# Holding the next head group's features behind the current group's triangular inverse

## The chip, the cores and the metric

The kernel runs on one core of a Trainium2 chip. The metric is the device time of one execution in microseconds, as the median of several runs; the times and the profile of the kernel before are shown below. Of the engines, TensorE is PE in the profile (its weight loads are PEld), VectorE is DVE, ScalarE is ACT, GpSimd is POOL and SyncE is SP.

## What is computed

The reference is a chain of two two-layer blocks on 256 tokens of width 1024. The change lies in the first block's second layer, a linear-attention mixer (RWKV) over 256 context tokens and then 256 latent tokens, in two directions:

```python
def wkv_scan(s0, decay, k, v, kk, a, r, reverse):
    def step(S, inp):
        w_t, k_t, v_t, kk_t, kka_t = inp[:5]
        S = (S * w_t[:, :, None, :]
             - jnp.einsum('bhij,bhj->bhi', S, kk_t)[..., None] * kka_t[:, :, None, :]
             + v_t[..., None] * k_t[:, :, None, :])
        y = jnp.einsum('bhij,bhj->bhi', S, inp[5]) if emit else None
        return S, y
```

with `decay = exp(-exp(-softplus(-w_raw) - 0.5))`, `a` a sigmoid of a low-rank product, 16 heads of width 64, and the scan of the context run first, so that its last state starts the scan of the latent tokens.

## The kernel before

The scan is done in blocks of 64 tokens, four to a sequence. There are four **head groups** g = 0 to 3: context of heads 0 to 7, latent tokens of the same heads, context of heads 8 to 15, latent tokens of those. Each group goes through four stages.

**Features** (`rw_feat`, L1079), in eight units: four head pairs hp by two directions d. A unit makes two low-rank products on PE (L1098), two tanh on ACT, then the decay sums L, a running sum of log decays on DVE (the scan at L1107), and from L the exponentials E3 and E2 (L1112, L1114, ACT). With them DVE builds the scaled keys BK (L1133, L1134) and queries ARx or ARc (L1136 to L1139). PE transposes BK (L1155), ACT copies that and its queue sends it to DRAM (kbd), PE multiplies BK by AR (L1165), and DVE masks the products into the group's matrix tile AB (L1178 for latent, L1183 for context groups); latent groups also make RB (L1181) and a bonus term (L1145 to L1150), and send ARx and RB to DRAM. In what follows a unit of a latent group is an x unit, one of a context group a c unit.

**Inverse** (`rw_inv`, L1194). It needs all eight units. ACT copies the diagonal 32 by 32 blocks of AB into ND (L1201, four copies), DVE transposes them (L1202), and then 31 dependent pairs of DVE instructions (L1210 multiply into xtmp, L1211 add into X) invert 64 triangular blocks at once. `F["inv"]` is the last of them.

**Post** (`rw_post`, L1214; `rw_post2`, L1242, for the last group). Two DVE transposes of X (L1219, L1221), ACT copies, and 32 by 32 matmuls on PE (L1231, L1237) finish the inverse of the 64 by 64 blocks, in two halves.

**Chain** (`rw_chain`, L1274). Four steps s. A step needs the state St of the step before and the finished AB: PE makes pR (L1303, L1310, in `begin`), ACT copies it to rhs (L1323), PE multiplies by AB to pU (L1329), ACT copies to UV (L1333), PE makes the next state (L1350), DVE scales it to St (L1357); latent groups also make the output pY. The last step of a group makes the pR of the next group's first step. Key blocks, and for latent groups ard and rbd, come back from DRAM for each step.

Between these, `tick` (L339) places **ticks** on PE: two matmuls of a modulation product for the second block (L247, `ada_wide`), each with a load of 512 KB of weights (wraw, issued from SP into two buffers). Ticks are anchored behind feature products and pU products, and come one after another in program order.

In the loop at L943 the code of a group is written as inverse, post, chain, and `ahead(p)` writes the units of the next group at the chain steps in `pos`. That is the order in which they are written. The order in which each engine runs them is set when the kernel is built, by a scheduler that may place an instruction earlier if its inputs and buffers are there. `self.after(i, prev)` is an edge that it must keep: i stands behind prev on its engine, or waits for it.

Of the kernel before, what the change touches and what calls it, by code (L numbers as in the profile page):

```python
# [13 lines left out]
ALU = mybir.AluOpType  # L14
# [6 lines left out]
S = 256  # L21
# [745 lines left out]
class L1(K):  # L767
# [14 lines left out]
    def odd1(self, xs, cst, Acol, Bcol):  # L782

        nc, A, tc = self.nc, self.A, self.tc
# [5 lines left out]
        J, mstrict, mincl, rmask = rc[:, 0:P], rc[:, P:P + 64], rc[:, P + 64:2 * P], rc[:, 2 * P:]  # L790
# [22 lines left out]
        for d in range(2):  # L813
            nc.gpsimd.memset(E3[d][:, :, 64 * d:64 * d + 1], 1.0)
        bon = self.T(rk, [P, 2, 16], "bon")
        E = dict(E3=E3, kT=kTd, kkn=kknd, rT=rTd, twl=twl, tal=tal, hpar=hpar, hka=hka, vd=vd, ms=mstrict, mi=mincl, rmask=rmask, bon=bon, rkI=rkI,
                 kbd=[self.tc.dram_tile([2, 4, P, 4, P], F32, name=f"kb_dram{g}") for g in range(4)],
                 ard=[self.tc.dram_tile([2, 4, P, 4, P], F32, name=f"ar_dram{g}") for g in range(2)],
                 rbd=[self.tc.dram_tile([2, 4, P, 8, 64], F32, name=f"rb_dram{g}") for g in range(2)])
        self.weights(2)  # L820
        with self.phase(ns2=6) as ph:
# [72 lines left out]
            F = self.rw_open(0, False, fp, fw)  # L894
# [38 lines left out]
        with self.phase((3, 2, 1), 0) as ph:  # L933
            self.pl = ph.es.enter_context(tc.tile_pool(name="pl", bufs=1, space=PSUM, reuse_waits="tile"))
            gp = ph.pool("gp")
            St = [self.T(gp, [P, 2, 4, P], f"St{c}") for c in range(2)]
            for c in range(2):
                nc.gpsimd.memset(St[c], 0.0)
            E.update(St=St, yd=yd, Y1=Y1)
            self.lo = "lo"  # L940
            self.at, self.side = "unit", self.late_side
            st = None
            for g in range(4):  # L943
                N = {"hp": 0}

                def ahead(p):

                    while g < 3 and N["hp"] < 4 and self.pos[g][N["hp"]] <= p:
                        if N["hp"] == 0:
                            N["F"] = self.rw_open((g + 1) // 2, g % 2 == 0, fp if g == 2 else gp, gp)  # L950
                        self.rw_feat(N["hp"], gp, E, N["F"])
                        N["hp"] += 1
                ahead(0)
                self.rw_inv(gp, F)
                ahead(1)
                rest = (self.rw_post2 if g >= self.g2 else self.rw_post)(gp, F)
                st = self.rw_chain(gp, E, F, st, ahead, rest)
                ahead(9)
                F = N.get("F")
                if F:  # L960
                    Fl = F
            F = Fl

            self.do(self.side)
            E.update(z=z, J=J, sgl=sgl, behind=F["inv"])
            sl = slice(512, 1024)
            nc.gpsimd.dma_start(lng1, A["lng"][sl].partition_broadcast(P))
            nc.gpsimd.dma_start(g21, A["g2"][:, sl])
            t2 = lambda n: self.T(gp, [P, 512], n, bufs=3 if n in ("BK", "ARx") else 2)
            lng, lnb, g2 = (t2("BK") for _ in range(3))  # L970
            nc.gpsimd.dma_start(lng, A["lng"][0:512].partition_broadcast(P))
            nc.gpsimd.dma_start(lnb, A["lnb"][0:512].partition_broadcast(P))
            nc.gpsimd.dma_start(g2, A["g2"][:, 0:512])
            for t in range(2):
                rows = slice(t * P, (t + 1) * P)
                y, y1 = t2("KB"), t2("ARx")
                nc.scalar.dma_start(z[:, t, :], vd[0][rows, 0:512])
                nc.scalar.dma_start(y, yd[0][rows, :])
                nc.scalar.dma_start(y1, yd[1][rows, :])
                self.rw_bonus(0, t, E, z[:, t, :], lnb)  # L980
                self.rw_readout(t, E, y, y1, t2("RB"), lng, g2, z[:, t, :])
            lnb = t2("BK")
            nc.gpsimd.dma_start(lnb, A["lnb"][sl].partition_broadcast(P))
            for t in range(2):
                nc.scalar.dma_start(z1[:, t, :], vd[0][t * P:(t + 1) * P, sl])
                self.rw_bonus(1, t, E, z1[:, t, :], lnb)
# [92 lines left out]
    def rw_feat(self, hp, gp, E, F):  # L1079
        nc = self.nc  # L1080
# [14 lines left out]
        for d in range(2):  # L1095
            pwa = self.T(self.pl, [P, 2, S], self.lo)
            for n, (w2, l) in enumerate(((w2s, E["twl"]), (a2s, E["tal"]))):
                i = mm(pwa[:, n, :], w2[:, hp, :], l[:, d, tok], start=True, stop=True)  # L1098
            self.tick(self.tk[0][F["g"]][d], i)
            tw = f1()  # L1100
# [3 lines left out]
            rev = slice(None, None, -1) if d else slice(None)  # L1104
            nc.scalar.activation(tw, tw, AF.Copy, bias=-0.5 * DT_C, scale=-0.5 * DT_C)
            L = f1()
            nc.vector.tensor_tensor_scan(L[:, rev], E["rmask"][:, 0:S], tw[:, rev], 0.0, ALU.mult, ALU.add)  # L1107
            E3 = E["E3"][d]
            lo, hi = (1, 65) if d == 0 else (0, 64)
            plo, phi = (0, 64) if d == 0 else (1, 65)  # L1110
# [51 lines left out]
            for c in range(4):  # L1162
                for h2 in range(2):
                    hs = slice(64 * h2, 64 * h2 + 64)
                    i = mm(pxs[h2][:, c, :], BK[hs, c, :], ar[hs, c, :], start=True, stop=True)  # L1165
# [1025 lines left out]
```

## Time and profile before

| | |
|---|---|
| median of 3 runs | 2179.67 us (2177.97 to 2191.19) |
| the profiled execution's own time | 2203.59 us |
| its span, first to last instruction | 2201.8 us |
| PE busy in the span | 2014.0 us (91%) |
| DVE busy | 1216.7 us (55%) |
| ACT busy | 832.7 us (38%) |
| mean granted TensorE clock | 0.929 of full speed |

The four groups' inverses, posts and chains take the stretch from 880.8 to 1238.0 us of the span. The first eight units are made earlier, behind other layers' matmuls. In the profile's windows one sees busy time by engine; a busy PE includes the latency of each matmul, so that a stretch of small dependent matmuls shows a busy PE too. PEclk is the share of full clock that was granted: 1.00 is 2.4 GHz and 0.50 is 1.2 GHz. In rows of the timeline, the bracket at the end is the time for which the engine was idle before the row and what ended it.

### The profile page before, as it was taken

How to read it: one execution, taken by the hardware profiler on the slowest of the kernel's cores; microseconds unless marked ns; L12 is line 12 of the kernel's file. 1: busy time of each engine (PE TensorE's matmuls, PEld its weight loads, DVE VectorE, ACT ScalarE, POOL GpSimd, SP SyncE). 2: the span in 40 equal slices, each digit the busy share in tenths (PEclk: the TensorE clock that was granted, in tenths of full speed). 3: DMA queues.
4: the chain of work that ended last, by engine and by line, in shares of the span. 5: the costliest groups of instructions: out<-in, count | busy, mean ns of one | idle time of the engine just before them, and what ended most of it. 6: DMA issues, size and time to landing. Idle time of an engine off the chain costs nothing. (4 is left out here: it accounts for less than half of the span.)

```text
span 2201.8 us, 32051 instructions
## 1 busy us (share of the span) xinstructions
PE 2014.0 (91%) x12738; PEld 1434.8 (65%) x12738; DVE 1216.7 (55%) x2508; ACT 832.7 (38%) x1609; POOL 123.8 (6%) x229
## 2 busy tenths in 40 slices
PE   7999899999989998899996789989989979999896
PEld 4864688888866477675655678979565449646442
DVE  2237565565676644875738465666663345664433
ACT  4334443322344355465433355453441123232211
POOL 1100000001112000000111000000000000000000
PEclk9999999999989999569988999999989999998898
DMA  7446223345542344547884735554627958452594
GB/s 299 134 164 263 80 112 143 142 160 187 201 139 77 116 145 145 170 133 247 274 256 127 266 122 187 198 197 157 249 88 282 378 193 313 168 230 96 201 379 166
DMA packets 124947, 417.44 MB, mean 190 GB/s; under 512 B 19536, under 2 KB 58096, under 8 KB 90096
## 3 DMA queue, kind: packets, MB, share of 16 engines
q1 hardware_dynamic: 54064, 314.86, 38.3%
q10 hardware_dynamic: 55552, 50.95, 7.5%
q0 software_dynamic: 15168, 49.44, 6.7%
q8 instruction: 104, 1.70, 0.3%
q14 instruction: 59, 0.48, 0.1%
HBM read 386.31 MB, written 28.89 MB: 189 GB/s over the span
## 5 line engine op out<-in xcount | busy, mean ns | idle before, releaser
L192 DVE TENSOR_TENSOR wlo<-wraw,whi 128x1024 fp32r<-128x1024 f32 x252 | 307.8, 1224 | 327.7 <-ACT whi L189 327.2
L189 ACT ACTIVATE whi<-wraw 128x1024 fp32r<-128x1024 f32 x252 | 265.6, 1058 | 495.5 <-PE mm L217 237.4
L215 PE MATMUL mm<-hT_h,whi 128*128 128x256 f32 (+1 forms) x832 | 267.9, 334 | 2.3 <-ACT whi L189 2.3
L216 PE MATMUL mm<-hT_l,whi 128*128 128x256 f32 (+1 forms) x832 | 268.1, 329 | 0.0
L217 PE MATMUL mm<-hT_h,wlo 128*128 128x256 f32 (+1 forms) x832 | 242.0, 327 | 2.1 <-DVE wlo L192 2.0
L215 PEld LDWEIGHTS mm<-hT_h,whi 128*128 128x128 f32 x832 | 157.5, 191 | 20.1 <-ACT whi L189 3.7
L216 PEld LDWEIGHTS mm<-hT_l,whi 128*128 128x128 f32 x832 | 158.9, 191 | 14.5
L217 PEld LDWEIGHTS mm<-hT_h,wlo 128*128 128x128 f32 x832 | 149.7, 191 | 18.3 <-DVE wlo L192 3.8
L216 PE MATMUL mm<-wlo,b 128*128 128x512 f32 x384 | 151.7, 395 | 0.6 <-DVE wlo L192 0.6
L217 PE MATMUL mm<-whi,b 128*128 128x512 f32 x384 | 151.3, 394 | 0.0
L2043 PE MATMUL ada<-wraw,mo_xd 128*64 128x512 f32 x512 | 135.5, 599 | 0.0
L215 PE MATMUL mm<-whi,b 128*128 128x512 f32 x384 | 135.5, 394 | 0.0
L247 PE MATMUL ada<-wraw,csil 128*32 128x512 f32 x512 | 99.1, 632 | 13.3 <-DMA wraw<-in_bdaU 11.7
L402 PE MATMUL tr<-s,x 128*128 128x128 f32 x288 | 56.7, 344 | 51.3 <-DVE s L393 25.8
L216 PE MATMUL mm<-wlo,hT_h 128*128 128x512 f32 (+1 forms) x256 | 100.3, 394 | 1.4 <-DVE wlo L192 1.4
L215 PE MATMUL mm<-whi,hT_h 128*128 128x512 f32 (+1 forms) x256 | 96.4, 403 | 2.0 <-ACT s L627 1.4
L217 PE MATMUL mm<-whi,hT_l 128*128 128x512 f32 (+1 forms) x256 | 96.7, 391 | 0.0
L402 PEld LDWEIGHTS tr<-s,x 128*128 128x128 f32 x288 | 49.5, 242 | 63.1 <-issue 37.5
L216 PEld LDWEIGHTS mm<-wlo,b 128*128 128x128 f32 x384 | 72.3, 188 | 18.7 <-DVE wlo L192 1.8
L215 PEld LDWEIGHTS mm<-whi,b 128*128 128x128 f32 x384 | 72.3, 188 | 16.7
L217 PEld LDWEIGHTS mm<-whi,b 128*128 128x128 f32 x384 | 72.3, 188 | 16.4
L2043 PEld LDWEIGHTS ada<-wraw,mo_xd 128*64 128x64 f32 x512 | 38.1, 136 | 67.9 <-issue 67.6
(544 smaller groups left out, 3717.7 us busy)
## 6 DMA issues: line engine op xcount, KB each, us to landing
wraw<-in_w SPq DMA_DIRECT2D x64, 1024.0 KB, 4.8
wraw<-in_moe_gu SPq DMA_DIRECT2D x64, 1024.0 KB, 8.1
wraw<-in_moe_d SPq DMA_DIRECT2D x32, 1024.0 KB, 7.6
PT<-in_adaT POOLq DMA_DIRECT2D x48, 512.0 KB, 4.9
wraw<-in_bdaU SPq DMA_DIRECT2D x48, 512.0 KB, 4.9
wraw<-in_bdaU SPq DMA_DIRECT2D x24, 1024.0 KB, 5.2
wraw<-in_adaU SPq DMA_DIRECT2D x16, 1024.0 KB, 7.6
wraw<-in_b_in SPq DMA_DIRECT2D x12, 1024.0 KB, 8.2
```

Of the source, the lines that this page charges most:

```text
L189: nc.scalar.activation(h, src, AF.Copy)
L192: self.low = nc.vector.tensor_tensor(l, src, h.bitcast(F32), ALU.subtract)
L215: mm(ps, ah, bh, start=first, stop=False)
L216: mm(ps, ah, bl, start=False, stop=False)
L217: mm(ps, al, bh, start=False, stop=last)
L247: i = nc.tensor.matmul(ps[q:q + 32, :], lhs[:, k, :], raw[:, c % self.wn, :], start=k == 0, stop=k == KT - 1, tile_position=(0, q))
L402: nc.tensor.matmul(pt[:, j, :], xs[e + j][:, k * P:(k + 1) * P], dall[:, e + j, :], start=True, stop=True)
L2043: nc.tensor.matmul(pg[64 * e:64 * e + 64, :], xd[:, k, s0:s0 + 64], gu[e](k), start=k == 0, stop=k == KT - 1, tile_position=(0, 64 * e))
```

## The change

Two lines hand the inverse's last instruction to the next group's features, and two order the scan of the decay sums behind it:

```diff
                         if N["hp"] == 0:
                             N["F"] = self.rw_open((g + 1) // 2, g % 2 == 0, fp if g == 2 else gp, gp)
+                            N["F"]["behind"] = F["inv"]
                         self.rw_feat(N["hp"], gp, E, N["F"])
...
             L = f1()
-            nc.vector.tensor_tensor_scan(L[:, rev], E["rmask"][:, 0:S], tw[:, rev], 0.0, ALU.mult, ALU.add)
+            i = nc.vector.tensor_tensor_scan(L[:, rev], E["rmask"][:, 0:S], tw[:, rev], 0.0, ALU.mult, ALU.add)
+            if F.get("behind") is not None:
+                self.after(i, F["behind"])
```

F is the current group and `N["F"]` the next one, so the 24 scans of groups 1, 2 and 3 stand behind the inverse of groups 0, 1 and 2. The first group's features carry no such edge. No instruction is added or taken away, and no size changes; lines below L1107 move down by three. The built order shows what else moves.

On DVE, in the first group's inverse, the kernel before has the scans and keys of group 1 (f, BK, ARx) between the pairs:

```order
L1210 TENSOR_TENSOR xtmp_6339<-NS_6309,X_6310 128x192
L1107 SCALAR_TENSOR_TENSOR f_1387_6697<-rwc_4530,f_1385_6692 128x256
L1211 TENSOR_TENSOR X_6310<-X_6310,xtmp_6339 128x24x8
L1210 TENSOR_TENSOR xtmp_6342<-NS_6309,X_6310 128x207
L1136 TENSOR_TENSOR ARx_6709<-kknl_6681,E_905_4556 128x2x128
L1137 TENSOR_TENSOR ARx_6709<-rTl_6683,E_905_4556 128x2x2x64
L1211 TENSOR_TENSOR X_6310<-X_6310,xtmp_6342 128x23x9
L1121 TENSOR_TENSOR f_1389_6703<-f_1389_6703,kTl_6679 128x256
```

The changed kernel has the 62 instructions of the inverse in one piece (these are the last three), and the same scan and keys behind them:

```order
L1214 TENSOR_TENSOR X_6310<-X_6310,xtmp_6405 128x2x30
L1213 TENSOR_TENSOR xtmp_6408<-NS_6309,X_6310 128x31
L1214 TENSOR_TENSOR X_6310<-X_6310,xtmp_6408 128x31
L1108 SCALAR_TENSOR_TENSOR f_1387_6697<-rwc_4530,f_1385_6692 128x256
L1222 STREAM_TRANSPOSE NS_6411<-X_6310 128x32x32
L1224 STREAM_TRANSPOSE ND_6413<-X_6310 128x32x32
L1139 TENSOR_TENSOR ARx_6709<-kknl_6681,E_905_4556 128x2x128
L1140 TENSOR_TENSOR ARx_6709<-rTl_6683,E_905_4556 128x2x2x64
```

The scan that stood at the eighth of the 31 pairs now stands behind the last, ahead of the two transposes that open the post. The second and third inverses read alike.

On DVE, around the second group's inverse (X_7448), the kernel before runs steps of the first group's chain (St) and masks of the group after next (AB_8193) between the pairs:

```order
L1211 TENSOR_TENSOR X_7448<-X_7448,xtmp_7498 128x17x15
L1210 TENSOR_TENSOR xtmp_7501<-NS_7447,X_7448 128x256
L1357 TENSOR_TENSOR St_1315_6304<-mm_6581,gC_5273 64x8x64 x2
L1211 TENSOR_TENSOR X_7448<-X_7448,xtmp_7501 128x16x16
L1210 TENSOR_TENSOR xtmp_7504<-NS_7447,X_7448 128x255
L1211 TENSOR_TENSOR X_7448<-X_7448,xtmp_7504 128x15x17
L1183 TENSOR_TENSOR AB_8193<-tr_8423,rwc_4530 128x2x2x64
```

In the changed kernel the last state of that chain (L1360) stands ahead of the last masks of group 1 (AB_6673), and the inverse's opening transpose (L1205) behind both:

```order
L1360 TENSOR_TENSOR St_1316_6305<-mm_7130,gC_5273 64x8x64 x2
L1181 TENSOR_TENSOR AB_6673<-tr_7362,rwc_4530 128x2x2x64
L1184 TENSOR_TENSOR RB_7376<-tr_7362,rwc_4530 128x4x64
L1153 COPY bon_4560<-tr_7410 128x2x2
L1181 TENSOR_TENSOR AB_6673<-tr_7421,rwc_4530 128x2x2x64
L1184 TENSOR_TENSOR RB_7440<-tr_7421,rwc_4530 128x4x64
L269 TENSOR_TENSOR bB_1364_6601<-ada_7046,bdab_17_110 128x8 x2
L269 TENSOR_TENSOR bA_1365_6602<-ada_7046,bdab_17_110 128x8 x2
L270 SCALAR_TENSOR_TENSOR bA_1365_6602<-bA_1365_6602,bng_18_112 128x16
L1181 TENSOR_TENSOR AB_6673<-tr_7422,rwc_4530 128x2x2x64
L1184 TENSOR_TENSOR RB_7440<-tr_7422,rwc_4530 128x4x64
L1205 STREAM_TRANSPOSE NS_7447<-ND_7446 128x1024
```

All four states of the first chain moved from inside and ahead of the second inverse to ahead of it; the third chain and the fourth inverse stand the same way, and the third inverse's ND copies stand on ACT behind the last UV of the second chain.

On PE, at the opening of the second group's post (post_7558), the kernel before has two ticks between its products, with products of the group after next (ARc_8503) and of the first chain (KBl) close by:

```order
L200 MATMUL mm_7105<-UV_7103,AB_5272 64x64
L1231 MATMUL post_7558<-NS_7549,AB_6673 32x32 x2
L247 MATMUL ada_6603<-wraw_6906,csil_16_107 32x512 x2
L1231 MATMUL post_7558<-NS_7549,AB_6673 32x32 x17
L247 MATMUL ada_6603<-wraw_6949,csil_16_107 32x512 x2
L1231 MATMUL post_7558<-NS_7549,AB_6673 32x32 x13
L1165 MATMUL tr_8516<-ARc_8503,BK_8502 128x64 x4
L1155 MATMUL tr_8551<-ident_67,BK_8546 128x128 x4
L200 MATMUL mm_7024<-UV_6868,KBl_7077 64x64 x8
```

In the changed kernel fourteen ticks in a row stand ahead of the same products, behind the last product of the first chain; the last three of them are shown, with what follows:

```order
L247 MATMUL ada_7058<-wraw_7328,csil_16_107 32x512 x2
L247 MATMUL ada_7058<-wraw_7371,csil_16_107 32x512 x2
L247 MATMUL ada_7058<-wraw_7431,csil_16_107 32x512 x2
L1234 MATMUL post_7558<-NS_7549,AB_6673 32x32 x17
L247 MATMUL ada_7058<-wraw_7435,csil_16_107 32x512 x2
L1234 MATMUL post_7558<-NS_7549,AB_6673 32x32 x15
L1099 MATMUL lo_8299<-twl_4544,w2s_8195 128x256
L1158 MATMUL tr_8231<-ident_67,BK_8226 128x128 x4
L1168 MATMUL tr_8239<-ARc_8227,BK_8226 128x64 x4
```

The whole order of PE from there on: 17 ticks stand in the first chain, 15 around the second inverse, 16 in the second chain, none behind it (before: 48 ticks, the last of them in the third chain). In each post that is followed by features 2 to 2.5 units stand between its first product and the chain's first pU, and the rest, 5.5 to 6, in the chain behind it; the last unit's products stand next to the chain's last step.

## Rows read from the trace of the kernel before

**Rows 1.** Windows by stage: stretch, length; busy by engine (instructions); PEclk, DMA share, GB/s.
```profile
880.80:942.20 61.40, 53.21 (x227) 41.57 (x226) 53.84 (x165) 30.08 (x85) 0.00 (x0) 0.56 0.59 174
942.20:977.10 34.90, 34.38 (x356) 28.63 (x354) 22.01 (x49) 27.80 (x58) 1.10 (x2) 0.50 0.26 78
977.10:1042.20 65.10, 59.19 (x831) 35.37 (x830) 44.11 (x114) 30.32 (x65) 4.28 (x8) 1.00 0.76 242
1042.20:1055.00 12.80, 12.33 (x171) 7.37 (x169) 6.18 (x16) 10.17 (x18) 1.11 (x2) 1.00 0.74 237
1055.00:1122.80 67.80, 62.82 (x799) 42.16 (x797) 46.82 (x124) 27.30 (x57) 8.43 (x16) 0.90 0.85 273
1122.80:1143.00 20.20, 18.07 (x260) 10.72 (x258) 3.75 (x11) 5.57 (x11) 3.01 (x6) 0.78 0.82 265
1143.00:1200.60 57.60, 40.20 (x658) 27.16 (x656) 45.37 (x101) 21.65 (x33) 9.16 (x17) 0.81 0.49 154
1200.60:1238.00 37.40, 30.20 (x674) 26.32 (x674) 8.79 (x15) 12.73 (x22) 2.12 (x4) 0.91 0.56 178
```
**Rows 2.** Windows of the four inverses, tile xtmp alone: stretch, length, DVE busy.
```profile
880.79:942.24 61.45, 20.59 (x62) 0.56 0.59 174
974.26:1011.10 36.84, 20.96 (x62) 0.96 0.77 243
1051.67:1108.99 57.32, 20.89 (x62) 0.94 0.87 276
1154.98:1183.67 28.69, 21.19 (x62) 0.85 0.50 161
```
**Rows 3.** Timeline of DVE: start, length, line, tiles.
```profile
887.03 0.69 DVE L1107 TENSOR_TENSOR_SCAN f<-rwc,f 128x256 f32<-128x256 f32 x1 [1.58 <-ACT f L1105]
...
942.28 2.07 DVE L1219 STREAM_TRANSPOSE NS<-X 128x1024 f32<-128x1024 f32 x1
944.20 1.92 DVE L1221 STREAM_TRANSPOSE ND<-X 128x1024 f32<-128x1024 f32 x1
...
1169.25 0.42 DVE L1210 TENSOR_TENSOR xtmp<-NS,X 128x255 f32<-128x255 f32 x1
1169.71 0.42 DVE L1211 TENSOR_TENSOR X<-X,xtmp 128x255 f32<-128x255 f32 x1
```
**Rows 4.** The copies into ND, line L1201: ns min/median/max, first and last start.
```profile
L1201 ACT ACTIVATE ND<-AB x16: 1052/1054/1056, 874.5 to 1150.6; 32x1024 f32<-32x1024 f32 x16
```
**Rows 5.** Timeline of PE at pU products, the first of chains 0, 1, 3.
```profile
977.13 1.14 PE L1329 MATMUL mm<-rhs,AB 64*64 64x64 f32 x30
...
1054.95 1.14 PE L1329 MATMUL mm<-rhs,AB 64*64 64x64 f32 x30
...
1200.62 1.09 PE L1329 MATMUL mm<-rhs,AB 64*64 64x64 f32 x30 [0.52 <-ACT rhs L1323]
...
1233.54 1.97 PE L1329 MATMUL mm<-rhs,AB 64*64 64x64 f32 x32 [0.75 <-ACT rhs L1323]
```
**Rows 6.** Windows of PE for L1165 (two stretches), L1098, L1155, L247, tile post.
```profile
977.10:1042.20 65.10, 7.94 (x72) 1.00 0.76 242
1055.00:1122.80 67.80, 11.06 (x72) 0.90 0.85 273
...
977.10:1042.20 65.10, 5.56 (x19) 1.00 0.76 242
...
977.10:1042.20 65.10, 2.62 (x16) 1.00 0.76 242
...
977.10:1042.20 65.10, 20.01 (x80) 1.00 0.76 242
...
977.10:1042.20 65.10, 5.06 (x192) 1.00 0.76 242
```
**Rows 7.** Ticks: PE's waits at L247 (us, times); the weights' DMA issues.
```profile
  DMA wraw<-in_bdaU: 27.1, 29
...
wraw<-in_bdaU SPq DMA_DIRECT2D x46, 512.0 KB, 5.0
```

## The prediction, made before the changed kernel was run

> **What bounds the kernel now.** I read the windows by stage first, because the change touches one sixth of the span. The four head groups take 880.8 to 1238.0 us, 357.2 us, and I cut them where one stage hands on to the next [rows 1]: inverse 0 (61.4), post 0 up to the chain's first pU (34.9), chain 0 (65.1), the wait for post 1 (12.8), chain 1 (67.8), the wait for post 2 (20.2), chain 2 with inverse and post 3 (57.6), chain 3 (37.4). The starts of chains 0, 1 and 3 are in [rows 5]. The reader is to see that in the first five stretches PE is busy nearly throughout (53 of 61, 34 of 35, 59 of 65, 12 of 13, 63 of 68 us): features, chain and ticks of different groups fill each other's waits. Only around chain 2 and 3 does PE stand (40 of 58, 30 of 37 us).
>
> Next come the windows of the inverses. Each holds 62 instructions with 20.6 to 21.2 us of work, but they last 61.5, 36.8, 57.3 and 28.7 us [rows 2], since DVE serves other work between the pairs. So the inverse is stretched, which is what the change removes; but the stretched inverses 1, 2 and 3 lie beside chains 0, 1 and 2 and beside the next features. Only inverse 0 has no chain beside it.
>
> **The change, part by part.** *What it gives.* An undisturbed inverse takes its 20.9 us and a gap per instruction: two neighbours in the last inverse start 0.46 us apart and take 0.42 [rows 3], so 62 times 0.04 comes on top, 23.4 us. Inverse 0 drops by 38 us.
>
> *What it takes.* Inverse g+1 needs every unit of group g+1, and no unit can pass its scan before inverse g has ended. From the built order, the last products of those units now stand next to the last step of chain g on PE, and PE and DVE run their rows in order. So inverse g+1 begins when chain g ends, and the post of g+1 and chain g+1 begin after it. The three later inverses come out from beside the chains and stand by themselves. The price of one: last masks 0.7 us (two DVE rows like the 0.42 us ones, in a pair), four copies into ND 4.2 [rows 4], the opening transpose 1.9 (the same form as L1221), 23.4, the scan that stands ahead of the transposes 0.6 (0.69 with overlap), and L1219 2.0 [rows 3]: **32.8 us** from the last feature to the post's first product. In this time PE has ticks at most.
>
> *Units.* On PE at full clock an x unit's products cost 11.06/4.5 = 2.46 us, a c unit's 7.94/4.5 = 1.76 (72 records, 16 to a unit); both add 5.56/4.75 = 1.17 for L1098, and 2.62/16 = 0.16 for each of three or four transposes [rows 6]: 4.1 and 3.6 us. A tick costs 20.01/20 = 1.0 us. The loads, stores and DMAs of the units move with them. They issue from ACT's queue, which they already shared with the chain's loads; POOL's KBl loads and SP's tick loads keep their order up to the last chain. I cost these at nothing; their cover is the chain, and where a late ard load shows it delays the ticks below.
>
> *The new sum, stretch by stretch.*
> - Inverse 0: 23.4.
> - Post 0: scan and transposes 4.6. Then PE at half clock, as in the row of before (0.50), where 30 us held the post and three c units. The post with 2.25 x units (the order has 2 to 2.5): 27. Together 31.6. Ends: 17, the last post, which took 1183.67 to 1200.62 with no features [rows 2, 5], and 35.5, as before.
> - Chain 0: from the row's 59.2 us busy I take its features (16.1), three ticks (3.0) and the pieces of post 1 (5.1), and add 5.75 x units (23.7): 58.7, with the row's 5.9 us of idle **64.6**. Ends: 55 (17 ticks at 3.25 us, 65.1/20) and 76 (19 us a step).
> - To chain 1: 32.8, and post 1 with 2.25 c units, 20 (ends 15 and 31). The fourteen ticks ahead of the post, with one inside it, need 15 loads of which two are there. With two buffers, a landing of 5.0 us [rows 7] and the tick, a load comes every 3.0 us: 13 times 3.0 and a last tick are 40 us, 7 more than the inverse hides; some of the post's products stand ahead of the last tick, so I take 5 (ends 0 and 12). Sum 57.8, where 12.8 stood.
> - Chain 1: 62.8 less 4.5 x units (18.5) and a piece of post (1.7), plus 5.75 c units (20.7) and 1.5 ticks: 64.9, with 5 us of idle 69.9; the last 6 lie behind the last feature and so beside inverse 2. 63.9. Ends 48 and 70.
> - To chain 2: 32.8 and post 2 with 2.25 x units, 24 (ends 15 and 31): 56.8, where 20.2 stood.
> - Chain 2: a bare step takes (1233.54 - 1200.62)/3 = 11 us [rows 5], one with features and ticks 65.1/4 = 16.3. With x units and no ticks I take 14.3, nearer to the second since the units are there, 57 in all (ends 44 and 76). Then 30.2 to the end of inverse 3, and 17 for its post. 104.2, where 57.6 stood.
> - Chain 3: 37.4 as before.
>
> The sum is 440.9 us against 357.2: **83.7 us more**. The profiled execution took 2203.59 us, 1.1% over the median of 2179.67; in the median's scale the loss is 82.8, and the time 2262.5, say **2263 us**. So the 38 us from inverse 0 are given back twice, before chain 1 (+45), and again before chain 2 (+37) and chain 3 (+47).
>
> The granted clock bears on this. From 880.8 to 977.1 it was 0.56 and 0.50, while PE was busy 88 of 96 us with features and post and no ticks; from 977 on, with ticks and chain, 1.00 [rows 1]. The Trainium skill ("TensorE: Matmul & The Clock Gate", section "HAM oscillation — how this bites in real kernels") says that an engine left waiting in each round starts every round throttled and pays again each time. That speaks against this change, which puts three more waits of 30 us on PE. By the row the throttled stretch is post 0 alone, as summed; by the rule posts 1 and 2 would be too, as in the third rival.
>
> **The rivals.**
> 1. *The chains run at their bare pace.* With the inverse gone from beside them, DVE answers at once, and chains 0 to 2 take 11 us a step with posts of 17: three rounds of post and chain of 61 us instead of my 89 on average. That is just the point at which the change costs nothing: the rest of the new sum (23.4, twice 32.8, 30.2, 17 and 37.4) leaves 184 us of the 357 to three rounds. For it: St waits behind inverse pairs in stretch 7, where PE idles 17 us. Against it: PE is busy 59 of 65 us in chain 0 at full clock, so it is PE and not DVE that sets 16 us a step there, and the units still have to pass. A quarter of the way up from there to the forecast the loss is 20 us: 2200 us, within 1%.
> 2. *Faster.* The units run ahead of the chain: if the eight of them are done early, inverse 1 ends before chain 0 does, and chain after chain follows without a wait. Then the inverse's 38 us remain as a gain: 2142 us. It decides at one point: whether the last unit's products come some 33 us before chain 0's last state. The order on PE puts them beside it; only a chain that itself runs 33 us late could bring this about.
> 3. *PE stays at half clock* in posts 1 and 2 and in chain 2, which has no ticks left. Posts 1 and 2 then cost post 0's 27 us instead of 20 and 24. Chain 2's units (23.7) and its other products (up to stretch 7's 40 us busy) would take longer, and the row's 17 us of idle absorb a part; I put 25 us on that. Together 35 us more: 2298 us. This is what the rule of the Trainium skill named above would do here; against it speaks that the clock was 0.81 in stretch 7 with few ticks [rows 1].
> 4. *The edge changes nothing*, because the scans would have stood there anyway: excluded by the order.
>
> **How the numbers follow.** My forecast, a loss of 30 to 130 us, has a chance of 0.78; the half clock 0.08, its time lying inside the same bounds; rival 1 0.09; faster 0.05. All lower ends together would give a loss of 10 us, all upper ends 148; half of the way to both is 46 and 116, and rival 3 fills the upper side. The range is 2210 to 2310 us. About 1% is what a measurement of this kernel can tell from no change: slower by over 1% is the forecast and the third rival, 0.86; within 1% 0.09; faster 0.05.
>
> **What the changed profile would show.** Four inverses of 23 to 25 us each, with no L1108 between the pairs. ND copies of inverse 1 that begin within some 5 us of chain 0's last state, and L1205 behind it. L247 waits for wraw beside inverse 1, with L1234 behind them. PE idle 20 us or more beside inverses 2 and 3. The time from the first inverse to the last pY near 441 us. I am wrong if an inverse begins while its predecessor's chain has a step or more to go, if post 1 starts less than 25 us behind chain 0's end, or if chains 0 to 2 take under 13 us a step.

## The result, and the profile after

The changed kernel takes **2270.06 us** (median of 4 runs, 2262.97 to 2284.7) where the kernel before takes 2185.07 (4 runs, 2177.97 to 2191.19). The ratio is **1.0399, with a 95% interval of 1.0331 to 1.0467**: 85 us slower. The forecast was 2263, between 2210 and 2310.

The profiled execution of the changed kernel took 2262.97 us, with a span of 2261.2. It was the fastest of its four, and that of before (2203.59 us) lay 0.8% above the median of 2185.07, so the two spans differ by only 59.4 us. Where I cut time into stretches, it is that pair, and it has to explain 59 us and not 85.

Windows by stage, cut as in [rows 1]: inverse 0, post 0, chain 0, the wait for chain 1, chain 1, the wait for chain 2, chain 2 with inverse and post 3, chain 3. Columns: stretch, length; busy time by engine (instructions); PEclk, DMA share, GB/s.

```profile
873.60:896.90 23.30, 4.82 (x38) 3.63 (x38) 21.20 (x63) 1.74 (x4) 0.00 (x0) 0.57 0.33 102
896.90:926.90 30.00, 26.97 (x319) 21.61 (x319) 20.64 (x49) 23.07 (x52) 1.11 (x2) 0.50 0.31 85
926.90:991.60 64.70, 58.23 (x660) 35.61 (x659) 26.06 (x68) 20.50 (x46) 3.21 (x6) 0.95 0.86 268
991.60:1051.80 60.20, 41.85 (x441) 18.25 (x440) 40.96 (x98) 25.24 (x55) 3.85 (x7) 0.79 0.56 183
1051.80:1107.50 55.70, 49.45 (x685) 34.58 (x686) 17.00 (x37) 21.13 (x48) 6.54 (x12) 1.00 0.84 265
1107.50:1164.50 57.00, 26.11 (x382) 20.64 (x382) 43.02 (x110) 25.12 (x50) 6.03 (x12) 0.58 0.31 97
1164.50:1255.90 91.40, 52.12 (x757) 39.06 (x758) 65.79 (x156) 35.84 (x71) 6.42 (x12) 0.78 0.43 124
1255.90:1295.20 39.30, 30.31 (x686) 26.93 (x682) 8.59 (x15) 12.50 (x22) 2.13 (x4) 0.87 0.52 170
```

Against [rows 1], inverse 0 lost 38.1 us and post 0 4.9, chain 0 stayed, and chain 1 lost 12.1. The two waits ahead of chains 1 and 2 grew by 47.4 and 36.8, the stretch with chain 2 by 33.8, chain 3 by 1.9. Together 421.6 us against 357.2: 64.4 more. Ahead of this the changed kernel is 7.2 us earlier, behind it 2.2 later. Differences of this size in one execution need no cause in the edit: inverse 0 begins anywhere from 871.1 to 881.4 us in the fourteen profiles of this document.

The four inverses, tile xtmp alone (stretch, length, DVE busy), which answer to [rows 2]:

```profile
873.60:896.90 23.30, 21.20 (x62) 0.57 0.33 102
996.20:1019.50 23.30, 21.21 (x62) 0.66 0.60 209
1115.40:1139.80 24.40, 21.17 (x62) 0.52 0.19 62
1216.70:1240.10 23.40, 21.23 (x62) 0.50 0.15 41
```

Each is now as short as its 62 instructions allow. That they nevertheless cost time is seen on DVE at the end of chain 0, around inverse 1 (timeline: start, length, line, tiles, and in brackets how long DVE had been idle and what ended it):

```profile
980.27 1.39 DVE L1360 TENSOR_TENSOR St<-mm,gC 64x512 f32<-64x512 f32 x2 [0.71 <-PE mm L200]
...
989.41 0.42 DVE L1181 TENSOR_TENSOR AB<-tr,rwc 128x256 f32<-128x256 f32 x1 [0.49 <-PE tr L1168]
...
994.16 1.94 DVE L1205 STREAM_TRANSPOSE NS<-ND 128x1024 f32<-128x1024 f32 x1 [3.99 <-ACT ND L1204]
996.20 0.20 DVE L1213 TENSOR_TENSOR xtmp<-NS,X 128x31 f32<-128x31 f32 x1
...
1019.46 0.68 DVE L1108 TENSOR_TENSOR_SCAN f<-rwc,f 128x256 f32<-128x256 f32 x1
1020.06 2.04 DVE L1222 STREAM_TRANSPOSE NS<-X 128x1024 f32<-128x1024 f32 x1
```

The last mask (L1181) waits for the last unit's products (L1168), the inverse follows, and the first held scan of group 2 (L1108) comes behind its last pair. All of it lies behind chain 0's last state (L1360). PE pays at the posts of groups 0, 2 and 3; the waits of PE in 873.6 to 1296.2 (line, releaser, us in total, times, longest):

```profile
PE post L1234 <- DVE NS L1222: 49.6, 2, 30.4
PE post L1264 <- DVE NS L1251: 25.6, 1, 25.6
PE ada L247 <- DMA wraw<-in_bdaU: 22.7, 17, 4.5
```

The 49.6 us are the 30.4 us at group 2's post and another 19.2 at group 0's. There, beside inverse 0, the held features have left PE almost nothing to do (4.82 us busy of 23.30), so the 38 us that inverse 0 lost were in part PE's work, which is now done later. The waits of the kernel before in its 880.8 to 1239.2, where no wait for an inverse is among the largest:

```profile
PE ada L247 <- DMA wraw<-in_bdaU: 11.7, 13, 2.7
PE mm L200 <- DVE St L1357: 9.3, 4, 6.2
```

The one ledger that holds all of it is PE's busy time over that whole region, from the first pair of inverse 0 to the last copy of Y1 (so a microsecond longer than my stages). Before:

```profile
880.80:1239.20 358.40, 310.40 (x3959) 219.30 (x3958) 230.87 (x591) 166.82 (x348) 29.22 (x54) 0.80 0.64 200
```

After:

```profile
873.60:1296.20 422.60, 289.86 (x3958) 200.31 (x3958) 243.27 (x591) 166.12 (x348) 29.28 (x54) 0.79 0.55 170
```

The same products take PE 20.5 us less, but it stands for 132.7 us where it stood for 48.0. The loss is waiting, and the clock hardly moved (0.80, 0.79).

### The profile page after: what moved, and what is told of

It is laid out like the page before. It is cut to its first block, busy times and chain, and to the rows that moved or that the text cites. A ratio compares the mean times of both kernels' runs of the same rounds, so it can differ in the third digit from the quotient of the medians.

```text
span 2261.2 us, 32065 instructions
## 1 busy us (share of the span) xinstructions
PE 1988.3 (88%) x12738; PEld 1412.3 (62%) x12738; DVE 1229.2 (54%) x2508; ACT 831.8 (37%) x1609; POOL 123.2 (5%) x229
## 5 line engine op out<-in xcount | busy, mean ns | idle before, releaser
L2046 PE MATMUL ada<-wraw,mo_xd 128*64 128x512 f32 x512 | 135.5, 599 | 0.0
L247 PE MATMUL ada<-wraw,csil 128*32 128x512 f32 x512 | 101.6, 658 | 25.0 <-DMA wraw<-in_bdaU 22.7
L402 PE MATMUL tr<-s,x 128*128 128x128 f32 x288 | 55.4, 337 | 51.5 <-DVE s L393 25.6
L2046 PEld LDWEIGHTS ada<-wraw,mo_xd 128*64 128x64 f32 x512 | 38.1, 136 | 67.9 <-issue 67.6
```

The lines of the kernel that those rows point to most:

```text
L247: i = nc.tensor.matmul(ps[q:q + 32, :], lhs[:, k, :], raw[:, c % self.wn, :], start=k == 0, stop=k == KT - 1, tile_position=(0, q))
L402: nc.tensor.matmul(pt[:, j, :], xs[e + j][:, k * P:(k + 1) * P], dall[:, e + j, :], start=True, stop=True)
L2046: nc.tensor.matmul(pg[64 * e:64 * e + 64, :], xd[:, k, s0:s0 + 64], gu[e](k), start=k == 0, stop=k == KT - 1, tile_position=(0, 64 * e))
```

## The experiments

Each run is read by three things, of which the third is the cost itself: how long each inverse lasts, how long it is from the first pair to the first pU, and how long from the last pU step of a chain to the first of the next one. Starts of pU steps are read from the timeline; a first pU starts with its main row of products, not with the few that can run ahead of it. Times in us; "region" as above, from one execution; the ratio is that of the timed runs to those of before on the same chip.

| kernel | inverses 0, 1, 2, 3 | to first pU | waits 0→1, 1→2, 2→3 | region | ratio, 95% interval |
|---|---|---|---|---|---|
| before | 61, 37, 57, 29 | 96 | 23, 34, 21 | 358.4 | |
| changed | 23, 23, 24, 23 | 53 | 79, 62, 55 | 422.6 | 1.040 (1.033 to 1.047) |
| e1_g1only | 23, 66, 34, 26 | 53 | 122, 14, 9 | 391.1 | 1.023 (1.017 to 1.029) |
| e2_g2only | 58, 26, 53, 26 | 79 | 24, 101, 11 | 402.1 | 1.032 (1.025 to 1.038) |
| e3_g3only | 61, 35, 28, 23 | 94 | 32, 17, 59 | 392.8 | 1.027 (1.020 to 1.033) |
| e4_pos2 | 23, 28, 31, 25 | 56 | 54, 41, 39 | 402.5 | 1.029 (1.021 to 1.036) |
| e5_after_short | 12, 12, 15, 12 | 42 | 66, 47, 48 | 374.6 | see there |
| e6_before_short | 27, 27, 25, 17 | 54 | 54, 26, 23 | 347.8 | see there |
| e7_edges12 | 23, 23, 50, 26 | 54 | 78, 84, 11 | 408.6 | 1.033 (1.028 to 1.038) |
| e8_mid | 47, 45, 58, 26 | 69 | 41, 75, 22 | 385.2 | 1.015 (1.010 to 1.020) |
| e9_small_loads | 23, 33, 24, 23 | 53 | 87, 70, 55 | 453.1 | 1.047 (1.044 to 1.050) |
| e10_before_pos2 | 59, 42, 45, 25 | 92 | 25, 14, 18 | 344.4 | 0.998 (0.994 to 1.002) |
| e11_mid_g1 | 47, 48, 53, 30 | 78 | 35, 34, 20 | 345.6 | 0.997 (0.994 to 1.001) |
| e12_two_of_four | 42, 49, 51, 26 | 70 | 50, 32, 22 | 354.2 | 1.003 (1.001 to 1.006) |

**One edge at a time.** The edge was kept for group 1, 2 or 3 alone:

```diff
-            if F.get("behind") is not None:
+            if F.get("behind") is not None and F["g"] == 1:
```

> The edge is kept for group 1's features alone (behind inverse 0); groups 2 and 3 are free as in the kernel before. Theory (an inverse that must wait for units tied to the end of a chain stands by itself and costs its own length): inverse 0 falls to 23 to 24 us and chain 0 starts some 40 us earlier, but inverse 1 then begins at chain 0's end and, with 14 scans of group 2 between its pairs, lasts about 50 us; the rest runs as before. Time 2190 to 2215 us (+5 to +30). Rival (the edge behind inverse 0 is pure gain, since no chain runs beside inverse 0, and the loss belongs to groups 2 and 3): 2145 to 2155 us. Rival (the clock): a half clock in post 1 and chain 1 that the kernel before does not have there.

> The edge is kept for group 2's features alone (behind inverse 1). Theory: inverse 0 stays near 61 us; inverse 2 begins at chain 1's end and stands by itself, with six scans of group 3 between its pairs, so that the wait before chain 2 grows from 20 us to 60 or more; inverse 3 stays beside chain 2. Time 2210 to 2245 us (+25 to +60). Rival (the cost of the three edges is one pile-up of ticks and the clock, not the inverses): within 10 us of before.

> The edge is kept for group 3's features alone (behind inverse 2). Theory: inverse 2 loses the x units between its pairs and falls from 57 us to some 30, which shortens the wait before chain 2; inverse 3 begins at chain 2's end and stands by itself, so that the stretch from chain 2's first pU to chain 3's grows from 58 us to about 90. Time 2185 to 2215 us (0 to +30). Rival (only the number of edges counts, a third of the loss for each): 2213 us.

Measured: 2240.05, 2262.5 and 2250.51 us, where before takes 2190.43 on that chip. All three lie above what I expected, and above every time that a rival names. Their losses (50, 72 and 60) add up to 182, twice that of the whole change; by the regions it is 33, 44 and 34, together 111 against 64. The inverses of e1_g1only and then of e2_g2only (tile xtmp, in order of the groups) show why:

```profile
880.20:903.50 23.30, 21.20 (x62) 0.57 0.31 97
1006.20:1071.70 65.50, 20.64 (x62) 0.84 0.73 226
```

```profile
957.90:984.00 26.10, 21.19 (x62) 0.87 0.58 191
1112.00:1164.90 52.90, 20.90 (x62) 0.56 0.67 193
```

With the edge on group 1 alone, inverse 1 begins 26 us behind the last pU step of chain 0 (979.6), about as in the changed kernel (24). But group 2's scans are free and go between its pairs, so it is late and lasts 65.5 us; the wait becomes 122 us. In return, the waits ahead of chains 2 and 3 fall to 14 and 9. So in e1, and likewise in e2, a single edge costs more than its share since the next group, which is not held, stretches the very inverse that the edge has put on the path. For e3 this is not the reason: inverse 3 has no next group and lasts 23 us. There the wait ahead of chain 3 grows from 21 to 59, about as in the changed kernel (55), and inverse 0, filled with group 1's features as before, gives nothing back: 94 us to the first pU, where e1 has 53. The clock rival of e1 is not out: post 1 and chain 1 (1071.7 to 1101.9 and 1101.9 to 1159.3) ran at a granted clock of 0.67 and 0.83, where before has 1.00 and 0.90, and no run separates that share of the loss.

**Edges on two groups.** `F["g"] < 3` in the same line, to test that reading:

> The edge for groups 1 and 2 only, group 3 free. If the costs of single edges added up (2240 and 2262 against 2185), this would be 2317, and over 2300 in any case. Theory (a late inverse costs its length, and it is long only where the next group's scans are free to stand between its pairs): inverse 1 is late and short (24 us instead of 65 with the edge on group 1 alone), inverse 2 is late and long (some 50 us, group 3's scans in it), inverse 3 not late (under 30 us from the last pU of chain 2 to the first of chain 3, where all edges give 55): 2250 to 2275.

Measured: 2262.5 us (before 2196.16). The costs of e1 and e2 don't add up. The inverses:

```profile
1002.20:1025.50 23.30, 21.21 (x62) 0.71 0.64 225
1121.00:1170.70 49.70, 21.02 (x62) 0.59 0.74 217
1192.10:1218.30 26.20, 21.26 (x62) 0.70 0.20 61
```

Inverse 1 is late and short, inverse 2 late and long, and chain 3 follows 11 us behind chain 2. This is what the reading asked for, place by place, and 2262.5 lies in the expected range.

**Shorter inverses in both kernels.** If inverses stand on the path, shortening them must pay, and more so after the change. The loop over the pairs was cut in the changed kernel and in that of before:

```diff
-        for t in range(31):
+        for t in range(16):
```

> The changed kernel with 16 pairs of DVE instructions in each inverse instead of 31 (the last 15 columns of the inverses are left out, so its numbers are not the reference's). 30 of 62 instructions are 11.3 of an undisturbed 23.3 us. Theory (each inverse stands on the path, with no chain beside it): inverses 0, 2 and 3 give back 11.3 us each; inverse 1 gives nothing as long as the row of ticks beside it lasts on for 10 us behind it. 34 us less than the changed kernel's 2270: 2236, between 2225 and 2245. Rival (the loss is in the half clock and in the new order of features, and inverses are mostly covered): under 15 us less, 2255 or more.

> The kernel before with the same cut (16 pairs in each inverse, the last 15 columns left out). Theory: only inverse 3 stands alone here (28.7 us), and gives some 11 to 14 us; inverse 0 is filled with features that PE needs 53 of 61 us for, and inverses 1 and 2 lie beside chains 0 and 1, so they give little. 10 to 20 us less than 2185: 2165 to 2175, so the gap between the two short kernels is 60 to 70 us where it is 85 with full inverses. Rival (inverses cost as much in both kernels): 30 us less or more, 2155 or below, and a gap that stays at 85.

The times, 2649.79 and 2636.7 us, can't be set beside the others: the second block chooses its experts by the values, and with these ones it makes 1280 products at L2043 (L2046 after) where it made 512. The expected totals fall with that; the region still tells. Region of the short changed kernel, and its inverses:

```profile
871.90:1246.50 374.60, 293.58 (x3958) 205.58 (x3958) 201.88 (x471) 166.26 (x348) 29.31 (x54) 0.79 0.61 191
...
871.90:884.00 12.10, 11.04 (x32) 0.64 0.61 189
977.40:989.50 12.10, 11.02 (x32) 0.50 0.59 206
```

Region of the short kernel before, and two of its inverses:

```profile
879.10:1226.90 347.80, 295.55 (x3958) 207.76 (x3958) 198.49 (x471) 165.50 (x348) 29.19 (x54) 0.83 0.66 206
...
879.10:906.30 27.20, 10.90 (x32) 0.56 0.54 161
967.50:994.10 26.60, 10.82 (x32) 1.00 0.86 279
```

The changed kernel's region falls by 48.0 us (422.6 to 374.6), that of before by 10.6 (358.4 to 347.8). Three of its inverses were cut by 11.2 (23.3 to 12.1) and one by 9.4 (24.4 to 15.0): 43 us of the 48. By place, the first pU comes 11 us earlier and the three waits are 13, 14 and 8 us shorter. So after the change all four are on the path, and the rival, under 15 us, is out. The regions of the two short kernels differ by 26.8 us, those of the full ones by 64.2. Which inverse the 10.6 us of before come from is not shown, and it need not be the last: the shorter inverse changed the built order too. Only four of the ten scans that stood in inverse 0 are left there, the first pU comes 42 us earlier, and the wait ahead of chain 1 grows by 31; the wait ahead of chain 3, behind the last inverse (28.7 to 16.6), did not shrink (21 to 23). I had expected inverse 1 of the short changed kernel to give nothing behind its ticks, 34 in all. It gave its share too, because the order changed there as well: eight ticks stand in a row ahead of post 1, where fourteen did, and the post starts 3 us behind NS (992.0, 995.2).

**The edge from the middle of the inverse.** `F["inv"]` is set at the sixteenth of the 31 pairs, first for all groups (e8), then for group 1 alone (e11):

```diff
-            F["inv"] = nc.vector.tensor_tensor(X[:, t + 1:32, 0:m], X[:, t + 1:32, 0:m], tv, ALU.add)
+            i = nc.vector.tensor_tensor(X[:, t + 1:32, 0:m], X[:, t + 1:32, 0:m], tv, ALU.add)
+            if t == 15:
+                F["inv"] = i
```

> The edge, for all groups, from the 16th of the 31 pairs instead of the last. Theory (what costs is that inverse g+1 begins only when chain g has ended): inverse 0 takes some 42 us, two to three units of the next group pass in its second half, and inverse 1 begins two steps before chain 0 ends; its end then lies less than 15 us behind that of the chain. The loss is far less than half of 85: 2190 to 2215. Rival (the loss is in proportion to how long scans are held): half of it, 2225 to 2235.

> The edge for group 1 alone, from the 16th of the 31 pairs. Theory (what costs is an inverse that begins when the chain ahead of it has ended): inverse 0 takes some 46 us (15 less), inverse 1 runs beside chain 0 but is stretched to 40 us or more by group 2's free scans; the time from the last pU of chain 0 to the first of chain 1 is 30 to 45 us (23 before, 122 with the edge from the last pair). Gain 15 to 25 at inverse 0, loss 10 to 25 there: 2180 to 2215. Rival (any held scan of group 1 costs): near the 2240 of the edge from the last pair, 2225 or more.

e8 took 2229.3 us, a loss of 33 against 2196.16, in the rival's range and not in mine. By place, the theory holds at inverse 1 and fails at inverse 2 (xtmp again):

```profile
957.30:1001.90 44.60, 21.00 (x62) 0.93 0.74 236
1081.00:1139.30 58.30, 20.87 (x62) 0.79 0.69 222
```

Inverse 1 begins 42 us ahead of chain 0's last pU step (999.1), and the wait falls from 79 to 41. Inverse 2 begins only 10 us ahead of chain 1's last pU step (1091.2), and is stretched to 58, so that wait is 75, more than with the full edge. I had looked at the first inverse only.

e11, without the edges on groups 2 and 3, took 2185.36 us against 2193.12: no loss. Its inverse 0 is 15 us shorter than before's, inverse 1 stands beside chain 0 at 964.4, and the wait is 35, where the same group held to the end (e1) had 122. Its rival, 2225 or more, is out.

**Half of the units.** The edge from the last pair, for group 1 and only for head pairs 2 and 3 (`and F["g"] == 1 and hp > 1`):

> The edge from the last pair, for group 1 alone, and there only for the head pairs 2 and 3: four units pass in inverse 0 as before, four are held. Theory as for the mid edge: inverse 0 takes 45 to 52 us, the four held units pass in post 0 and chain 0's first half, inverse 1 runs beside chain 0 and the wait between the chains is 20 to 40 us: 2170 to 2205, within 1% of before. Rival (the held units are the last ones that inverse 1 needs, so it is as late as with all eight held): 2225 or more.

Measured: 2197.69 us against 2193.12, within the expected range of times; the wait of 50 us is longer than I had it (20 to 40), and inverse 0 shorter (42, not 45 to 52). Four free units suffice for inverse 1 to run beside chain 0 (968.7 to 1017.7, the last pU step at 998.4). So, for this group, holding scans is not what costs. What costs is to hold so many that the next inverse can't begin while the chain runs.

**Units written earlier.** With the full edges, and then without any, every unit is written at the third step of the chain ahead:

```diff
-    pos = ((3, 4, 9, 9), (9, 9, 9, 9), (4, 9, 9, 9), (5, 9, 9, 9))
+    pos = ((2, 2, 2, 2), (2, 2, 2, 2), (2, 2, 2, 2), (5, 9, 9, 9))
```

> All three edges are kept; the places at which the next group's units are written move from the chain's later steps to its first step, so that the built order puts all eight scans ahead of the chain's third state, and inverses 1 to 3 have two or three states of the chain between their pairs. Theory (the loss is that inverses stand by themselves because the units end with the chain): inverses stay at 23 to 28 us, the next inverse begins 30 us or more before the chain's end, and 50 to 90 us of the loss come back: 2175 to 2220 us. Rival (the edge itself costs, by the clock, PE's idle time at each inverse or the ticks): 2245 us or more.

> The kernel before, without any edge, with every unit written at the third step of the chain: the control of the changed kernel with the same numbers (2248, ratio 1.029). Theory (those numbers give the edge back some 20 us because the held units come earlier; without the edge nothing holds them): no gain here, 2180 to 2215. Rival (the numbers are better whatever the edge): 20 us less than before, 2160 to 2170.

Measured: 2248.29 with the edges, 2182.45 without them, where before takes 2190.43 and 2193.12. The control is as fast as before, so the earlier writing gives back a quarter of the loss only where the edge is there. I had hoped for more (2175 to 2220); 2248 lies in the rival's range. One premise did not come about: inverse 1 of e4 begins at 978.9, 13 us ahead of chain 0's last pU step (991.7) and not 30. The other was incomplete. The three waits are 61 us shorter together than in the changed kernel, but the chains, from first to last pU step, are 38 us longer together (chain 0's first step takes 28.2 us, against 17.5). The units that now pass earlier in the chains are the likely reason.

**Finer loads for the ticks.** The row of ticks ends 10 us behind inverse 1 in the changed kernel:

```profile
1030.45 1.92 PE L247 MATMUL ada<-wraw,csil 128*32 128x512 f32 x4 [0.45 <-DMA wraw<-in_bdaU]
1032.31 1.17 PE L1234 MATMUL post<-NS,AB 32*32 32x32 f32 x34
```

NS (L1222) had been there since 1022.1. The loads were halved, with twice the buffers:

```diff
-        self.wn = 2
+        self.wn = 1
-        self.weights(2)
+        self.weights(4)
```

> The changed kernel with the ticks' weights in loads of 256 KB into four buffers instead of 512 KB into two; the same weights in all. Theory (the row of ticks ahead of post 1 ends some 10 us behind inverse 1 because a load comes only every 2.5 to 3 us and just two are ahead): with finer loads the row keeps its pace nearer to the DMA's, ends 0 to 6 us behind inverse 1, and the time falls by 4 to 10 us: 2260 to 2266. Rival (the row is bound by what the DMA engines can bring, not by the two buffers): the row ends 10 us behind as before, 2270.

Measured: 2300.21 us against 2193.12. The ratio is 1.047 where the changed kernel has 1.040; the two intervals overlap, so it is not shown to be slower still, but the gain is out, and no theory had the region 30.5 us longer. The ticks' waits for weights from chain 0 to chain 1 did fall, from 19.2 us to 11.3, and PE then waits 6.4 for inverse 1, so the overhang is gone. But the built order changed: an instruction of the modulation (L284), which needs the ticks' sums, now stands among the pairs of inverse 1:

```profile
1035.41 0.32 DVE L1213 TENSOR_TENSOR xtmp<-NS,X 128x156 f32<-128x156 f32 x1
1044.27 0.69 DVE L284 TENSOR_TENSOR adb<-ada,adb 128x512 f32<-128x512 f32 x1 [8.55 <-PE ada L247]
1044.88 0.31 DVE L1214 TENSOR_TENSOR X<-X,xtmp 128x156 f32<-128x156 f32 x1
```

DVE waits 8.55 us for PE in the middle of the inverse. The Trainium skill ("TensorE: Matmul & The Clock Gate", section "Architectural detail: the array is 16× 32×32, not 1× 128×128") calls DVE's queue a strict FIFO; the trace agrees, since the inverse's 11 instructions behind L284 all wait. Chain 0 is slower too (pU steps of 26, 18 and 15 us against 18, 14 and 15), with ticks that keep PE busy for 26.0 us with 60 products where it was 12.6 with 52. A single product is about as long (619 ns on average, 605 in the changed kernel), so they overlap less; why stays open, and so does what the overhang costs by itself.

## Why the prediction came out, step by step

**The mechanism was right.** Inverse g+1 became an interval that stands alone between two chains, three times, and against the 38 us of inverse 0 (61.4 predicted to become 23.4; 23.3 measured) stand 47, 37 and 34 us at those places. The loss appears when the next inverse can't run beside the chain (e1, e2, e3, e7), all but vanishes when it can (e11, e12), and shrinks with the length of the inverses (e5). That it vanishes is shown for group 1's edge alone; e4, in which later inverses overlap their chains a little, kept most of its loss in slower chains.

**The terms that held.** Post 0: 31.6, measured 30.0. Chain 0: 64.6 and 64.7. To chain 1: 57.8 and 60.2. To chain 2: 56.8 and 57.0. The 32.8 us from the last feature product to the post's first one came out as 32.7 up to the end of NS at inverse 1, 34.9 at inverse 2 and 32.2 at inverse 3. Here is inverse 2 on PE:

```profile
1106.83 0.66 PE L1168 MATMUL tr<-ARc,BK 64*128 64x64 f32 x4
...
1110.95 1.05 PE L247 MATMUL ada<-wraw,csil 128*32 128x512 f32 x4
1142.43 1.92 PE L1234 MATMUL post<-NS,AB 32*32 32x32 f32 x64 [30.43 <-DVE NS L1222]
```

**The terms that didn't.** Two were too large, by 8.2 and 12.8 us. Chain 1 was to take 63.9 and took 55.7. I had taken its other work from the busy time in [rows 1], at a PEclk of 0.90; after the change the stretch ran at 1.00, and its ticks took 11.6 us (56 products) where they had taken 16.6 (58). A busy time was carried over as if the clock belonged to the work. The stretch with chain 2 was to take 104.2 and took 91.4: I chose 14.3 us a step, "nearer to the second" bound, and it took 12.0 from first to last pU step (1164.5 to 1200.5). One term was too small: the ticks' overhang ahead of post 1 was 10.2 us and not 5. Half of that is hidden in the sum, since NS was ready 30.5 us behind the stretch's start and not 32.8, and post 1 took 19.5. The stage terms as I gave them add up to 439.7, not the 440.9 that I wrote; measured is 421.6.

**So the sum was 18 us too large, and the time was hit all the same.** The sum's 82.5 stood against 64.4 in the profiled pair, and against 85 in the timed runs. In each of the ten experiments with a ratio, the timed loss exceeds the difference of the regions too, by 6 to 25 us (e1: 0.0227 times 2190.43 is 50, against 33; e11: -6 against -13). This fits a profiled execution of before that was some 15 us longer than usual; I had scaled for its 1.1% only in the last step, by 0.9 us, instead of asking in which stretch it lay. That is argued, not shown, but three kernels that take the same time as before within 0.3% (e10, e11, e12) have regions that are 14, 13 and 4 us shorter than its 358.4. The two largest excesses, of e2 and e3, lie mostly elsewhere: behind the region these took 979 and 978 us where before took 963. There, in the second block's attention, the granted clock was lower, as 100 us show that begin 670 us behind the region's end (before, then e2; columns as above):

```profile
1909.00:2009.00 100.00, 94.43 (x564) 46.75 (x557) 67.67 (x244) 34.25 (x133) 5.20 (x8) 0.90 0.50 198
1951.00:2051.00 100.00, 94.80 (x474) 43.43 (x467) 58.41 (x210) 27.20 (x111) 5.26 (x8) 0.73 0.48 187
```

PE is busy for as long, with 474 products instead of 564. So some 16 us of those two losses do not lie at an inverse; why the clock is lower there stays open. The closeness of 2263 to 2270 owes something to chance.

**The rivals.** Rival 1 (bare pace) holds for chain 2 alone, near 12 us a step, and so the sign that I had named against myself, a chain under 13, did appear there; chains 0 and 1 took 15.2 and 17.1. Rival 2 (units run ahead) did not come about; e11 and e12 are what it looks like, and even there it gives nothing that can be measured. Rival 3 was the half clock. By windows of posts 1 and 2, the first 15.5 us of chain 2, and post 3:

```profile
1032.30:1051.80 19.50, 18.45 (x370) 14.30 (x368) 11.27 (x26) 14.06 (x36) 2.78 (x5) 0.95 0.43 129
1142.40:1164.50 22.10, 21.61 (x312) 18.16 (x312) 15.19 (x38) 17.67 (x38) 1.11 (x2) 0.51 0.36 101
1164.50:1180.00 15.50, 11.73 (x155) 9.59 (x155) 10.87 (x28) 9.25 (x24) 1.07 (x2) 1.00 0.51 146
1242.10:1255.90 13.80, 9.60 (x156) 5.92 (x158) 12.39 (x21) 10.41 (x17) 0.54 (x1) 0.50 0.08 20
```

Post 1, with ticks through the wait ahead of it, ran at 0.95 (beside inverse 1 itself, where PE waits for the ticks' weights again and again, it was 0.66). Posts 2 and 3, behind waits of 30.4 and 25.6 us in which PE did nothing, ran at half clock, 0.51 and 0.50. For these two the trace agrees with the rule of the Trainium skill ("TensorE: Matmul & The Clock Gate", section "HAM oscillation — how this bites in real kernels") that the prediction names. Post 2 took 22.1 us up to its chain's pU, where I had 24, so the price was small, and chain 2 was back at 1.00 at once (third row).

**The signs.** Inverses of 23 to 25 us, L247 waiting for wraw beside inverse 1 with L1234 behind it, and PE idle beside inverses 2 and 3: seen. ND copies within 5 us of chain 0's last state: they came 9.6 us behind it (980.27, 989.87), since the last unit's products, not the state, release them. The time from the first inverse to the last pY, forecast near 441 us, was 421.6.

## What to carry to other kernels

Before lengthening the hold on a prerequisite, ask what the next stage needs in order to begin and whether it would still begin beside something: in this kernel a stretched piece of work beside a chain cost nothing that the time shows (e11, e12), while a short one between two chains cost its whole length (e5). Costs of such holds did not add up here, for each one changed how long the next piece lasted; test them together as well as singly. And a busy time taken from a row at a mixed clock belongs to that clock, not to the work.

## What the runs showed of the hardware

The same stretch of features can run near either of the two levels of the clock, 1.2 and 2.4 GHz. Inverse 0 with group 1's features (ten scans in both) is at a PEclk of 0.56 in the kernel before [rows 1], with PE busy 53 of 61 us, none of it ticks. In e10 it is at 0.94, with 56 tick products (15.4 us) added:

```profile
871.10:930.50 59.40, 50.27 (x274) 29.72 (x274) 55.32 (x172) 31.57 (x90) 0.00 (x0) 0.94 0.91 283
```

It takes 59.4 us instead of 61.4 although it holds these ticks as well. So the busy PE was not the bound there; DVE, busy for 53.8 of 61.4 and 55.3 of 59.4 us, is nearest to one. A busy PE at half clock can look like a bound where there is slack. I had read it as one in the prediction's first paragraph.
